# An encoder layer on one core: other Strassen product orders, sums seeded by ScalarE, and four buffers for turning the last rows

## The chip, the core and the metric

The kernel runs on one core of a Trainium2 chip. The metric is the device time of one execution in microseconds (us); lower is better. The time given is the median of three runs.

The core's engines each have an instruction queue of their own, in order: TensorE (PE: matmuls, with the weight loads listed apart as PEld), VectorE (DVE), ScalarE (ACT), GpSimd (POOL) and SyncE (SP), which here issues nearly all DMA transfers. On-chip data lies in SBUF; matmuls write PSUM, of which this kernel uses eight banks of 128 x 512 floats.

## The reference, cut

One layer of an encoder on x of 2048 rows and 1024 columns, all in float32:

```
h  = rms_norm(x, norm_mix)
z  = h @ w_in                       # q, k, v of two attentions, two gates
y_a = windowed_gqa(...)             # attention A
y_b = neighborhood_attn(...)        # attention B
merged = sigmoid(g_a + b) * (y_a @ w_proj_a) + sigmoid(g_b + b) * (y_b @ w_proj_b)
x  = x + merged @ w_out             # w_out is 1024 x 1024
h2 = rms_norm(x, norm_mlp)
x  = x + square(relu(h2 @ w_up)) @ w_down      # 1024 -> 4096 -> 1024
return rms_norm(x, norm_final)
```

## The kernel before

**Matmuls.** A float32 product is made from three reduced-precision (fp32r) matmuls: each operand is split into a high part, cast by ScalarE (L280), and a low part, a subtraction on VectorE (L281); `mm3s` (L283 to L286) issues high x high, high x low, low x high. The large products besides take one level of Strassen in Winograd's form: of an operand's four quarters, sums are made (`add`, L277, on VectorE), and seven products, numbered n = 1 to 7, replace eight. A list of orders says in which sequence the seven run; the results come from sums of products, which are kept in PSUM banks (matmuls accumulate there) or read out by VectorE and ScalarE.

**Stages on PE, in time:** the dense stage (h @ w_in, to about 365 us), attention A and B, the gated projections (to about 1175 us) with w_out beside them (its first half m=0 at about 1175 to 1250 us, its second, m=1, at about 1333 to 1418 us), up (to 2070 us), down.

**Dense stage.** `QUADS` lists its column groups; q counts them. `in_left` makes and splits the seven left operands of a group from its weights; the seven right operands, made from the normalised rows, are shared by the groups. `in_quad` (from L463) runs seven products in `ORDER`, each in two halves a of 128 columns, 12 matmuls a half. Banks are x, y, z, two each: x takes products 1 and 2, z takes 5 and 3, y takes 6, 7 and 4. Product 1 is copied out by ScalarE into c1 (L484), and VectorE adds c1 to what it reads from y and z, five adds a half (L277). A result goes through `in_result` (L440) to DRAM; if it is still in PSUM, ScalarE copies it (L454) into an `in_e` tile, of which there are two, or it is split for q and k (`qk_parts`, L423 to L430).
Beside these groups the rows x are normalised and turned for later use (squares L223, scaling L235, `turned_out`), and `wo_parts` (from L623) makes the seven right operands of w_out, split, into DRAM (wo_d).

**w_out.** `out_operands` (L1330) loads w_out's split operands back from wo_d (`pgl`, L1338, 1 MB each), and makes and splits those of the merged rows (the tiles m0 to m3). `out_products` (from L1352) runs the seven products in `ORDER_O = (1, 2, 5, 6, 7, 4, 3)`, each with four tiles t of 128 rows: product 1, once both contraction halves h are in, is copied by ScalarE into a y bank (L1378) and the rest accumulate onto it; the rows of x (`xr` tiles, from `x_row`) take the sums by VectorE's adds. Each m gives two row blocks, rows[0] and rows[1], of 512 rows. A finished block goes to DRAM (x2d), is normalised in place (`normalised`, ScalarE L223 and L235) and then turned out.

**Turning rows out.** `turned_out` (L240) takes a quarter g of a block: four 32 x 32 transposes on VectorE (L247), a multiplication by the gain (L252), and four stores of 128 KB through SP's queue (L255) into h2d, which up reads back. Its tile `ht` has one buffer. The blocks of m=0 are turned during the gated products of m=1; those of m=1 by `turned_last`: block 1 at step 6 of w_out's m=1 (in `beside_out`, L1399), block 0 after the loop (L1474 on).

**Up.** `up_start` (L1316), run beside w_out's m=1, loads up's first operands (w_up, and rows from h2d: `uraw`, `urb`). `up_right` (L1183) makes the seven right operands `ubh` (bh1 to bh7), `up_left` the left ones (`uwhla`, `uwhlb`), with sums in `uS`; `up_quad` (L1253) runs the products 1, 5, 6, 2, 7, 4, 3. `up_homes` (L1086) gives a right operand its place in SBUF, and so sets which older tiles must be done with before it can be written: bh6, bh3, bh2, rb and c are placed after the w_out loop; chunk, bh7 and bh4 after the last turned block, when w_out's tiles are closed.

**What sets the order.** The program is written as generators that run side by side (`beside`, `prep`, `started`), and a scheduler then orders each engine's queue within the dependencies, so the place of an instruction in a queue need not be that in the source. Every engine takes its queue in order: an instruction that waits holds up those behind it.

Of the kernel before, what the change touches and what calls it, by code (L numbers as in the profile page):

```python
# [92 lines left out]
def encoder_layer(ctx, tc, x, norm_mix, w_in, b_gate, sink, rpb, w_pa, w_pb, w_out,  # L93
# [275 lines left out]
    def in_left(ws, w, skip=()):  # L369
# [8 lines left out]
        for n in ORDER:  # L378
# [67 lines left out]
    def in_result(col, b, src, in_psum):  # L446
# [5 lines left out]
        if in_psum:  # L452
            t = in_e()[:, 0]
            A.copy(t, src)  # L454
            src = t
# [7 lines left out]
    def in_quad(c, w, lf, right, ybanks=ypool, zbanks=zpool):  # L463
# [4 lines left out]
        for n in ORDER:  # L468
            hl, (rh, rl) = next(lf), right[n]
            for a in range(na):  # L470
# [27 lines left out]
                elif n == 3:  # L498
                    add(V, u2[a], ps, u2[a])
                    in_result(first, 1, u2[a], False)  # L500
            yield
# [122 lines left out]
    def wo_parts(k, own):  # L624
# [5 lines left out]
        x1, x2 = rows  # L630
        b11, b12, b21, b22 = (r[:, j * BT : (j + 1) * BT] for r in rows for j in range(2))
        x3, t4 = own(), in_c()
        add(V, x3[:, 0:BT], b12, b11, ALU.subtract)
        add(V, x3[:, BT : 2 * BT], b22, b12, ALU.subtract)
        add(V, b12, b22, x3[:, 0:BT], ALU.subtract)
        add(V, t4, b21, b12, ALU.subtract)
        yield
        for ns, src in (((5, 7), x3), ((1, 6), x1), ((2, 3), x2), ((4,), t4)):
            hi = in_c() if len(ns) == 1 else in_e().rearrange("p a b -> p (a b)")
            A.copy(hi.bitcast(F32R), src)  # L640
            V.tensor_tensor(out=src.bitcast(F32R), in0=src, in1=hi, op=ALU.subtract)
            for j, n in enumerate(ns):
                for z, t in enumerate((hi, src)):
                    SY.dma_start(wo_d[n][k // 2, k % 2][:, z], t[:, j * BT : (j + 1) * BT])
# [10 lines left out]
    for q in range(2, len(QUADS)):  # L655
# [12 lines left out]
        lf = list(in_left(ws, 256, (1, 2) if q == 2 else ()))  # L668
# [8 lines left out]
        for n, _ in enumerate(quad2 if q == 2 else in_quad(*QUADS[q], iter(lf), right)):  # L677
# [638 lines left out]
    def up_start():  # L1316
# [3 lines left out]
        started.extend((rights, lf))  # L1320
# [3 lines left out]
        next(rights)  # L1324
        yield
        yield from up_left_steps(ws, lf)

    ORDER_O = (1, 2, 5, 6, 7, 4, 3)
    last_left = [None]
# [22 lines left out]
    def out_products(m, operands, rows, beside):  # L1352
# [4 lines left out]
        for n in ORDER_O:  # L1357
# [4 lines left out]
            for h in range(2):  # L1362
                l, r = ready[h]
                for t in range(4):
# [10 lines left out]
                    xc = None if n in (1, 5) else rows[i][t][:, j * BT : (j + 1) * BT]  # L1375
# [3 lines left out]
                    elif xc is not None:  # L1379
                        add(V, xc, ps, xc)  # L1380
                    if n == 7:
                        add(V, xc, z[t], xc)
                    if n in (4, 3):
                        put(x2d[2 * m + i][t * P : (t + 1) * P], rows[i][t])
                        flush(1)
            if n == 4:
                flush()
                normalised(p4x, rows[1], p4x, by_scalar=True, small=True)
        flush()
        normalised(p4x, rows[0], p4x, by_scalar=True, small=True)  # L1390

    def beside_out(m):

        loads = load_y(1) if m == 0 else up_start()
        for n in range(7):
            if n == 2 and m == 1:
# [293 lines left out]
```

## Time and profile before

| | us |
|---|---|
| median of 3 runs | 2686.42 |
| the runs | 2685.76 to 2692.47 |
| the profiled execution | 2692.09 |
| its span on the core | 2690.3 |
| PE busy | 2582.1 (96%) |
| VectorE busy | 1657.0 (62%) |
| ScalarE busy | 1258.4 (47%) |
| GpSimd busy | 352.3 (13%) |

The profile was taken of one execution, which is 5.7 us longer than the median; the 1.8 us between its span and its time lie around the span. A row of a group gives line, engine, operation, output <- input and count, then busy time, mean of one in ns, and the idle time just before with what ended it. A row of waits gives who waited for whom, then total, number and longest. A row of windows gives the stretch and its length, each engine's busy time in it with the number of instructions, the clock granted to PE (1.00 is full), the share of DMA engines busy, and GB/s. "SPq" is SP's queue issuing a DMA.

### The profile page before, as it was taken

How to read it: one execution, taken by the hardware profiler on the slowest of the kernel's cores; microseconds unless marked ns; L12 is line 12 of the kernel's file. 1: busy time of each engine (PE TensorE's matmuls, PEld its weight loads, DVE VectorE, ACT ScalarE, POOL GpSimd, SP SyncE). 2: the span in 40 equal slices, each digit the busy share in tenths (PEclk: the TensorE clock that was granted, in tenths of full speed). 3: DMA queues.
4: the chain of work that ended last, by engine and by line, in shares of the span. 5: the costliest groups of instructions: out<-in, count | busy, mean ns of one | idle time of the engine just before them, and what ended most of it. 6: DMA issues, size and time to landing. Idle time of an engine off the chain costs nothing.

```text
span 2690.3 us, 34393 instructions
## 1 busy us (share of the span) xinstructions
PE 2582.1 (96%) x12044; PEld 2142.4 (80%) x12044; DVE 1657.0 (62%) x2643; ACT 1258.4 (47%) x2245; POOL 352.3 (13%) x433
## 2 busy tenths in 40 slices
PE   7999999999999999999994999999999999999998
PEld 6878777787888888878873888888887888888887
DVE  7876756666444444466675767785666634545767
ACT  7344346666555555344343554554444233323444
POOL 0000123334555541000000000000000000000001
PEclk9999999999999999999997999999999999999999
DMA  5677685446776655777665665764435935445555
GB/s 180 228 248 202 212 284 151 118 116 174 209 228 191 195 159 150 256 242 237 227 251 160 205 214 204 253 246 145 162 114 206 347 131 172 143 149 171 179 191 170
DMA packets 351725, 525.93 MB, mean 195 GB/s; under 512 B 28584, under 2 KB 172072, under 8 KB 349376
## 3 DMA queue, kind: packets, MB, share of 16 engines
q1 hardware_dynamic: 344640, 506.95, 58.8%
q10 hardware_dynamic: 6912, 16.78, 1.7%
q8 instruction: 95, 1.56, 0.2%
q14 instruction: 78, 0.64, 0.1%
HBM read 349.51 MB, written 174.13 MB: 195 GB/s over the span
## 4 chain that ended last, share of the span: by engine, by line
PE 80%; DMA 8%; DVE 6%; ACT 2%; issue 1%; SPq 1%; POOL 0%; DVEq 0%; POOLq 0%; ACTq 0%
PE b L285 16%; PE b L286 16%; PE b L284 16%; PE mm L200 4%; PE mm L201 4%; PE mm L202 4%; PE av L984 2%; PE b L202 2%; PE b L200 2%; PE b L201 2%; PE s L945 2%; PE pt L973 2%; PE zb L284 1%; PE zb L286 1%; PE zb L285 1%
## 5 line engine op out<-in xcount | busy, mean ns | idle before, releaser
L285 PE MATMUL b<-dwh,dah 128*128 128x512 f32 x896 | 348.7, 389 | 0.4 <-DVE dwh L281 0.4
L286 PE MATMUL b<-dwh,dah 128*128 128x512 f32 x896 | 347.8, 389 | 0.0
L284 PE MATMUL b<-dwh,dah 128*128 128x512 f32 x896 | 338.3, 389 | 1.7 <-ACT dwh L280 1.7
L280 ACT CAST dah<-da 128x1024 fp32r<-128x1024 f32 (+1 forms) x128 | 120.8, 945 | 368.3 <-PE b L286 246.5
L281 DVE TENSOR_TENSOR dah<-da,dah 128x1024 fp32r<-128x1024 f32 (+1 forms) x128 | 139.2, 1089 | 216.5 <-ACT dah L280 216.3
L285 PE MATMUL b<-ubh,uwhlb 128*128 128x512 f32 x592 | 231.4, 391 | 30.6 <-DVE ubh L281 30.6
L284 PE MATMUL b<-ubh,uwhlb 128*128 128x512 f32 x592 | 231.6, 392 | 9.4 <-ACT ubh L280 7.8
L286 PE MATMUL b<-ubh,uwhlb 128*128 128x512 f32 x592 | 230.4, 391 | 0.0
L200 PE MATMUL mm<-hT,whl 128*128 128x512 f32 x544 | 218.9, 402 | 0.0
L202 PE MATMUL mm<-hT,whl 128*128 128x512 f32 x544 | 215.0, 395 | 0.0
L201 PE MATMUL mm<-hT,whl 128*128 128x512 f32 x544 | 214.3, 394 | 0.0
L284 PE MATMUL zb<-zh,zwhl 128*128 128x512 f32 x476 | 188.3, 397 | 15.7 <-DVE zc L277 8.5
L284 PEld LDWEIGHTS b<-dwh,dah 128*128 128x128 f32 x896 | 168.1, 188 | 37.0 <-ACT dwh L280 2.1
L285 PEld LDWEIGHTS b<-dwh,dah 128*128 128x128 f32 x896 | 168.2, 188 | 35.7 <-DVE dwh L281 0.8
L286 PEld LDWEIGHTS b<-dwh,dah 128*128 128x128 f32 x896 | 168.2, 188 | 34.9
L285 PE MATMUL zb<-zh,zwhl 128*128 128x512 f32 x476 | 187.4, 394 | 0.0
L286 PE MATMUL zb<-zh,zwhl 128*128 128x512 f32 x476 | 184.3, 393 | 0.8 <-DVE zwhl L281 0.8
L277 DVE TENSOR_TENSOR uc<-b,uc 128x512 f32<-128x512 f32 x160 | 109.3, 689 | 122.0 <-PE b L286 111.0
L285 PEld LDWEIGHTS b<-ubh,uwhlb 128*128 128x128 f32 x592 | 111.6, 189 | 54.6 <-DVE ubh L281 31.3
L284 PEld LDWEIGHTS b<-ubh,uwhlb 128*128 128x128 f32 x592 | 111.8, 189 | 33.6 <-ACT ubh L280 8.2
L1580 POOL TENSOR_TENSOR st<-st,power 128x1 f32<-128x1 f32 x16 | 13.6, 859 | 896.5 <-DVE st L1579 896.3
L286 PEld LDWEIGHTS b<-ubh,uwhlb 128*128 128x128 f32 x592 | 111.7, 189 | 23.1
(263 smaller groups left out, 5906.9 us busy)
## 6 DMA issues: line engine op xcount, KB each, us to landing
at<-uc SPq DMA_DIRECT2D x224, 256.0 KB
da<-at SPq DMA_DIRECT2D x96, 512.0 KB
dw<-in_w_down_dram SPq DMA_DIRECT2D x160, 256.0 KB
uraw<-in_w_up_dram SPq DMA_DIRECT2D x32, 1024.0 KB
pgl<-wo_d SPq DMA_DIRECT2D x28, 1024.0 KB
raw<-in_w_in_dram SPq DMA_DIRECT2D x34, 512.0 KB
zraw<-in_w_in_dram SPq DMA_DIRECT2D x16, 1024.0 KB
z<-zg SPq DMA_DIRECT2D x64, 256.0 KB
```

Source lines behind the costliest of these rows:

```text
L200: PE.matmul(ps, lh, rh, start=first, stop=False)
L201: PE.matmul(ps, lh, rl, start=False, stop=False)
L202: PE.matmul(ps, ll, rh, start=False, stop=last)
L277: return eng.tensor_tensor(out=out, in0=a, in1=b, op=op).ins
L280: A.copy(hi, src)
L281: return eng.tensor_tensor(out=lo, in0=src, in1=hi.bitcast(F32), op=ALU.subtract).ins
L284: PE.matmul(ps, lh, rh, start=first, stop=False, skip_group_check=True)
L285: PE.matmul(ps, lh, rl, start=False, stop=False, skip_group_check=True)
L286: PE.matmul(ps, ll, rh, start=False, stop=last, skip_group_check=True)
L945: PE.matmul(ps[:, :n], q[:, i, :], kv[:, z, B_R0[i] // 4 : (B_R0[i] + B_NR[i]) // 4, 4 * B_C0[j] : 4 * (B_C0[j] + w)], start=z == 0, stop= ...
L973: PE.transpose(pt[:kp, at + (i - i0) * P : at + (i - i0 + 1) * P], s[i][:, rr : rr + kp], ident)
L984: last = PE.matmul(po[:, i0 * P : (i0 + ni) * P], v[:kp, c, :], src[:kp, o : o + ni * P], start=first, stop=(c == 7 and z == 1), skip_grou ...
```

## The change

- **Dense stage, q = 3 to 8:** `in_quad` gives way to `in_seeded`, with the order 1, 5, 6, 2, 7, 3, 4. ScalarE copies product 1 into the y bank, onto which 6, 7 and 4 accumulate; products 5 and 6 are copied out by ScalarE (into c22 and u2); VectorE makes two adds a half instead of five. Results 2 and 4 are read from PSUM, and such copies go to `in_c` (ten buffers) instead of `in_e`. The group q = 2 keeps its order.
- **`wo_parts`:** splits each product by itself in pieces of 512 columns, its high parts in `in_c` tiles. It issues as many DMAs as before.
- **w_out:** `ORDER_O` becomes 1, 2, 5, 6, 3, 7, 4. Product 5 is added to the rows at once. Block 0 is complete after product 3, block 1 after product 4; which block is loaded and turned first follows.
- **Beside m=1:** x rows of block 1 are loaded at steps 0 and 1, up's first loads at steps 2 to 4. At step 6 block 0 is turned into four buffers, the halves of m2 and m3.
- **After the loop:** block 1 is turned through `hu`, a ring of four buffers. The homes change: bh3 is now placed after that block, and the addresses of bh2, bh3, bh4, bh7, rb, c and chunk are others. bh6 lies over m2 and m3, bh7 over the `hu` buffers, bh4 over the first of them and row tiles, bh3 over row tiles.

```diff
@@ -366,7 +366,7 @@
 
     last_part = [None]
 
-    def in_left(ws, w, skip=()):
+    def in_left(ws, w, skip=(), order=ORDER):
 
         a11, a21 = ws[0][:, :, 0:w], ws[0][:, :, w : 2 * w]
         a12, a22 = ws[1][:, :, 0:w], ws[1][:, :, w : 2 * w]
@@ -375,7 +375,7 @@
             return left_parts(src, w, eng)
 
         s1, s2 = None, None
-        for n in ORDER:
+        for n in order:
             if n in skip:
                 continue
             if n == 5:
@@ -450,7 +450,7 @@
                 SY.dma_start(dst, t)
             return
         if in_psum:
-            t = in_e()[:, 0]
+            t = in_c()
             A.copy(t, src)
             src = t
         if is_v(col):
@@ -498,6 +498,45 @@
                 elif n == 3:
                     add(V, u2[a], ps, u2[a])
                     in_result(first, 1, u2[a], False)
+            yield
+
+    ORDER_3 = (1, 5, 6, 2, 7, 3, 4)
+
+    def in_seeded(c, w, lf, right):
+
+        x, y, z = [None] * 2, [None] * 2, [None] * 2
+        u2, c22 = [None] * 2, [None] * 2
+        for n in ORDER_3:
+            hl, (rh, rl) = next(lf), right[n]
+            for a in range(2):
+                if n == 1:
+                    x[a] = zbank(xpool[a])
+                elif n == 5:
+                    z[a] = zbank(zpool[a])
+                ps = {1: x, 2: x, 5: z, 3: z, 6: y, 7: y, 4: y}[n][a]
+                at = slice(a * P, (a + 1) * P)
+                for k in range(4):
+                    mm3s(ps, hl[:, 0, k, at], hl[:, 1, k, at], rh[:, k], rl[:, k], k == 0 and n in (1, 5), k == 3)
+                first, second = c + a * P, c + w + a * P
+                if n == 1:
+                    y[a] = zbank(ypool[a])
+                    A.copy(y[a], ps)
+                elif n == 5:
+                    c22[a] = in_c()
+                    A.copy(c22[a], ps)
+                elif n == 6:
+                    u2[a] = in_c()
+                    A.copy(u2[a], ps)
+                elif n == 2:
+                    in_result(first, 0, ps, True)
+                elif n == 7:
+                    add(V, c22[a], ps, c22[a])
+                    in_result(second, 1, c22[a], False)
+                elif n == 3:
+                    add(V, u2[a], ps, u2[a])
+                    in_result(first, 1, u2[a], False)
+                elif n == 4:
+                    in_result(second, 0, ps, True)
             yield
 
     def scaled(out, ps, k):
@@ -627,21 +666,27 @@
         for p, r in enumerate(rows):
             SY.dma_start(r, w_out[0][(4 * p + k) * P : (4 * p + k + 1) * P, :])
         yield
-        x1, x2 = rows
         b11, b12, b21, b22 = (r[:, j * BT : (j + 1) * BT] for r in rows for j in range(2))
-        x3, t4 = own(), in_c()
-        add(V, x3[:, 0:BT], b12, b11, ALU.subtract)
-        add(V, x3[:, BT : 2 * BT], b22, b12, ALU.subtract)
-        add(V, b12, b22, x3[:, 0:BT], ALU.subtract)
-        add(V, t4, b21, b12, ALU.subtract)
-        yield
-        for ns, src in (((5, 7), x3), ((1, 6), x1), ((2, 3), x2), ((4,), t4)):
-            hi = in_c() if len(ns) == 1 else in_e().rearrange("p a b -> p (a b)")
+        t1, t3 = (t[:, j * BT : (j + 1) * BT] for t in (own(),) for j in range(2))
+
+        def part(n, src):
+            hi = in_c()
             A.copy(hi.bitcast(F32R), src)
             V.tensor_tensor(out=src.bitcast(F32R), in0=src, in1=hi, op=ALU.subtract)
-            for j, n in enumerate(ns):
-                for z, t in enumerate((hi, src)):
-                    SY.dma_start(wo_d[n][k // 2, k % 2][:, z], t[:, j * BT : (j + 1) * BT])
+            for z, t in enumerate((hi, src)):
+                SY.dma_start(wo_d[n][k // 2, k % 2][:, z], t)
+
+        add(V, t1, b12, b11, ALU.subtract)
+        yield
+        add(V, t3, b22, b12, ALU.subtract)
+        part(1, b11)
+        yield
+        add(V, b12, b22, t1, ALU.subtract)
+        part(3, b22)
+        yield
+        add(V, b11, b21, b12, ALU.subtract)
+        for n, src in ((2, b21), (5, t1), (7, t3), (6, b12), (4, b11)):
+            part(n, src)
             yield
 
     def own_v():
@@ -665,7 +710,7 @@
             xp = pools(s_z, "right", ("xin", "st"), "x2")
         if q == 7:
             bias_tables()
-        lf = list(in_left(ws, 256, (1, 2) if q == 2 else ()))
+        lf = list(in_left(ws, 256, (1, 2) if q == 2 else (), ORDER if q == 2 else ORDER_3))
         if q + 1 < len(QUADS):
             ws = in_weights(*QUADS[q + 1])
         if q in (5, 6):
@@ -674,7 +719,7 @@
             xt = x_tiles(xp, b, 3)
             normalised(xp, xt, Junk(), by_scalar=True)
         ops2.extend(lf if q == 2 else ())
-        for n, _ in enumerate(quad2 if q == 2 else in_quad(*QUADS[q], iter(lf), right)):
+        for n, _ in enumerate(quad2 if q == 2 else in_seeded(*QUADS[q], iter(lf), right)):
             next(prep, None)
             if q in (5, 6) and n < 4:
                 turned_out(h1d[b - 2], in_e().rearrange("p k x -> p (k x)"), xt, n)
@@ -1317,16 +1362,18 @@
 
         up_homes("raw", "whla", "whlb", "bh1", "bh5", "S")
         rights, lf = up_right(0), {}
-        started.extend((rights, lf))
+        next(rights)
+        yield
         next(rights)
         ws = up_weights(0)
         yield
-        next(rights)
-        yield
-        yield from up_left_steps(ws, lf)
-
-    ORDER_O = (1, 2, 5, 6, 7, 4, 3)
-    last_left = [None]
+        rest = up_left_steps(ws, lf)
+        started.extend((rights, lf, rest))
+        for _ in range(2):
+            next(rest)
+        yield
+
+    ORDER_O = (1, 2, 5, 6, 3, 7, 4)
 
     def out_operands(ms):
 
@@ -1372,47 +1419,44 @@
                     if h == 0:
                         continue
                     i, j = {1: (0, 0), 2: (0, 0), 5: (1, 1), 6: (0, 1), 7: (1, 1), 4: (1, 0), 3: (0, 1)}[n]
-                    xc = None if n in (1, 5) else rows[i][t][:, j * BT : (j + 1) * BT]
+                    xc = None if n == 1 else rows[i][t][:, j * BT : (j + 1) * BT]
                     if n == 1:
                         y[t] = bank_at(t)
                         A.copy(y[t], ps)
-                    elif xc is not None:
+                    else:
                         add(V, xc, ps, xc)
-                    if n == 7:
-                        add(V, xc, z[t], xc)
                     if n in (4, 3):
+                        i = int(n == 4)
                         put(x2d[2 * m + i][t * P : (t + 1) * P], rows[i][t])
                         flush(1)
-            if n == 4:
+            if n in (4, 3):
                 flush()
-                normalised(p4x, rows[1], p4x, by_scalar=True, small=True)
-        flush()
-        normalised(p4x, rows[0], p4x, by_scalar=True, small=True)
+                normalised(p4x, rows[int(n == 4)], p4x, by_scalar=True, small=True)
 
     def beside_out(m):
 
         loads = load_y(1) if m == 0 else up_start()
         for n in range(7):
-            if n == 2 and m == 1:
-                rows[1].extend(x_row(m, 1, t) for t in range(4))
-            if n in ((1, 3, 4, 6) if m == 0 else (0, 1, 3, 4)):
-                y = next(loads)
-                if m == 0:
-                    state["y"] = y
-            if m == 1 and n == 6:
-                turned_last(1)
+            if m == 0 and n in (1, 3, 4, 6):
+                state["y"] = next(loads)
+            elif m == 1:
+                if n < 2:
+                    rows[1].extend(x_row(m, 1, 2 * n + t) for t in range(2))
+                elif n < 5:
+                    next(loads)
+                elif n == 6:
+                    free = [T(p4x, [P, 2, 2, BT], F32, f"m{t}", 1).rearrange("p a b c -> p a (b c)") for t in (2, 3)]
+                    turned_last(0, lambda g: free[g // 2][:, g % 2])
             yield
-        if m == 1:
-            started.append(loads)
 
     def x_row(m, i, t):
         row0 = (2 * m + i) * BT + t * P
         return load_tile(p4x, "xr", 8, xf[row0 : row0 + P])
 
-    def turned_last(i):
+    def turned_last(i, own):
 
         for g in range(4):
-            turned_out(h2d[2 + i], T(p4x, [P, 2 * BT], F32, "ht", 1), rows[i], g, gain)
+            turned_out(h2d[2 + i], own(g), rows[i], g, gain)
 
     state = {"y": next_y}
     rows = None
@@ -1448,7 +1492,7 @@
             gated(f, 0)
         for f in range(8):
             if m:
-                i = 1 - f // 4
+                i = f // 4
                 turned_out(h2d[i], T(p4x, [P, 2 * BT], F32, "ht", 1), old[i], f % 4, gain)
             if 0 < f and f + early < 8:
                 gated(f + early, 0)
@@ -1457,7 +1501,7 @@
             if f == 3:
                 ready = [next(operands), next(operands)]
             if f >= 4 or m == 0:
-                rows[1 - f // 4].append(x_row(m, 1 - f // 4, f % 4))
+                rows[1 - f // 4 if m else f // 4].append(x_row(m, 1 - f // 4 if m else f // 4, f % 4))
         if m == 1:
             s_pg.close()
             s_w.close()
@@ -1471,16 +1515,18 @@
     for _ in beside:
         pass
     s_m.close()
-    up_homes("bh6", "bh3", "bh2", "rb", "c")
+    up_homes("bh6", "bh2", "rb", "c")
+    s_hu = ExitStack()
+    hu = ring(s_hu, "hu", [P, 2 * BT], F32, 4, "left")
     rights, lf, rest = started
     for _ in range(2):
         right = next(rights)
     for _ in rest:
         pass
-    turned_last(0)
+    turned_last(1, lambda t: hu())
+    s_hu.close()
     s_wo.close()
-
-    up_homes("chunk", "bh7", "bh4")
+    up_homes("bh7", "bh4", "bh3", "chunk")
     for m in range(2):
         if m:
             right = next(rights)
```

The orders of the queues that result differ in the dense groups q = 2 to 8 and the first part of attention A, in w_out's m=1 and in the first products of up. PE has as many instructions as before; VectorE has 2621 instructions in place of 2645, ScalarE 1989 in place of 1943; GpSimd and SP have as many as before (438 and 1525).

## The prediction

> **What bounds the kernel now.** I read the page from the top: the span, the engines, then the busy tenths in 40 slices of 67 us.
>
> ```profile
> span 2690.3 us, 34393 instructions
> ...
> PE 2582.1 (96%) x12044; PEld 2142.4 (80%) x12044; DVE 1657.0 (62%) x2643; ACT 1258.4 (47%) x2245; POOL 352.3 (13%) x433
> ...
> PE   7999999999999999999994999999999999999998
> ```
>
> PE (the matmul engine) bounds it: busy 2582.1 of 2690.3 us, so 108 us idle, and the change removes no matmul. It can win only idle PE time and the slower clock behind an idle stretch. In the slices one digit falls to 4 after the start: slice 22, about 1412 to 1480 us, where w_out ends and "up" begins. So I asked for PE's waits: total, times, longest; first over the span, then from 120 to 366 us, the dense groups q=3 to 8.
>
> ```profile
> PE b L285 <- DVE ubh L281: 32.1, 2, 30.6
> ...
> PE b L284 <- ACT ubh L280: 7.8, 1, 7.8
> PE b L284 <- DMA pgl<-wo_d: 5.0, 2, 3.2
> ```
>
> ```profile
> PE zb L284 <- DVE zc L277: 7.2, 4, 3.5
> PE zb L284 <- ACT zwhl L280: 4.2, 1, 4.2
> PE zb L395 <- ACT ze L454: 0.8, 1, 0.8
> ```
>
> Three places carry the change: the border w_out/up (30.6 + 7.8 us), the DMA wait in w_out, and 12.2 us in the dense groups.
>
> **The border first, as it holds most.** Busy time by 10-us stretches (columns: PE, PEld, DVE, ACT, POOL, granted clock, DMA share, GB/s):
>
> ```profile
> 1430.00:1440.00 10.00, 7.59 (x33) 5.59 (x31) 10.00 (x15) 7.06 (x8) 1.98 (x2) 1.00 0.59 159
> 1440.00:1450.00 10.00, 1.22 (x2) 0.50 (x2) 8.40 (x11) 3.36 (x5) 0.00 (x0) 0.63 0.92 259
> 1450.00:1460.00 10.00, 0.00 (x0) 0.00 (x0) 2.65 (x5) 0.00 (x0) 0.00 (x0) 0.50 0.47 137
> 1460.00:1470.00 10.00, 0.00 (x0) 0.00 (x0) 4.42 (x10) 0.00 (x0) 0.00 (x0) 0.50 0.34 76
> 1470.00:1480.00 10.00, 1.24 (x3) 1.05 (x4) 5.80 (x8) 0.00 (x0) 0.00 (x0) 0.50 0.39 80
> 1480.00:1490.00 10.00, 10.00 (x38) 7.98 (x38) 6.86 (x8) 5.58 (x8) 0.00 (x0) 0.82 0.80 246
> ```
>
> PE idles 2.41 + 8.78 + 10 + 10 + 8.76 = 39.95 us here; then it runs at half clock: 1.24 us x 0.5 = 0.6 and 10 x 0.18 = 1.8. Lost: **42.4 us**. VectorE is two thirds idle meanwhile. What it does stands in its timeline (start, length, instruction, idle before and who ended it) and the chain of work that ended last (start, length, what):
>
> ```profile
> 1461.57 1.42 DVE L247 STREAM_TRANSPOSE ht<-xr 128x256 f32<-128x256 f32 x4 [4.01 <-DMA h2d<-ht]
> 1463.02 1.23 DVE L252 TENSOR_TENSOR ht<-ht,gt 128x1024 f32<-128x1024 f32 x1
> 1468.19 1.43 DVE L247 STREAM_TRANSPOSE ht<-xr 128x256 f32<-128x256 f32 x4 [3.95 <-DMA h2d<-ht]
> ...
> 1477.49 2.35 DVE L281 TENSOR_TENSOR ubh<-uraw,ubh 128x1024 fp32r<-128x1024 f32 x2
> ```
>
> ```profile
> 1465.12 0.47 SPq L255
> 1465.63 2.48 DMA h2d<-ht
> ```
>
> Turning a row out takes 1.42 + 1.23 = 2.65 us of VectorE per quarter, but a quarter comes round every 1468.19 - 1461.57 = 6.62 us: `ht` is one buffer, and each quarter waits until the last of its four stores (0.47 us to issue, 2.48 to land) has landed. Both last rows go through it, eight quarters, and VectorE's queue holds the low half (L281) of product 6's operand behind them. That is the stall.
>
> **Border, after.** turned_last(0) moves to the last step of w_out, into halves of m2 and m3; turned_last(1) follows the loop, in four `hu` buffers. No quarter waits for a store any longer: a row is 4 x 2.65 = 10.6 us of VectorE instead of 4 x 6.62 = 26.5. I set t = 0 at the end of w_out on PE. Products 1 and 5 of up run first: by the rate of a full stretch (next fence: 46 matmuls in 10 us) 96 matmuls take 20.9 us. The last row's adds and scaling reach VectorE at about t = 13 (before: PE stops at about 1439 behind these two products, so w_out ended at about 1418; the last scaling was issued at 1432.45 and took 2.19 for two).
>
> ```profile
> 1420.00:1430.00 10.00, 10.00 (x46) 8.28 (x45) 4.16 (x8) 8.08 (x16) 0.55 (x1) 1.00 0.79 249
> ```
>
> ```profile
> 1432.45 2.19 ACT L235 ACTIVATE xr<-xr,st 128x1024 f32<-128x1024 f32 x2
> ```
>
> Now what is late next, product by product; all four are estimates, bounded below by 0 (the operand is there) and above by the whole row in front of it (10.6):
> - Product 6: home bh6 lies on m2/m3, free only after the 16 stores of turned_last(0): 16 x 0.47 = 7.5 us of SP's queue, plus 2.48. These begin before t = 0, so its low half is last, with part of a turned quarter (2.65) ahead: 1.7 taken.
> - Product 2: its low half stands behind the gains of the `hu` quarters: one quarter, 2.5.
> - Product 7: bh7 lies on `hu`, so its ScalarE cast (1.04) waits for the last store: 4 issues x 0.47 + 2.48 + 1.04 = 5.4, of which some 2 us lie beside product 2: 3.5.
> - Product 4: three 1.2-us VectorE steps (sums for the next weights, splits) stand ahead of its own, 3.7 in all, little covered: 4.0.
>
> Together 11.7 us, and one half-clock spell of 1.7 us (worked out below): 13.4. **Border: 13.4 - 42.4 = -29**, between -40 (next to no waits) and -17 (the four at twice the size, 23.4, and the one spell). Up's own work and the row order inside m=1 do not change the count of VectorE's adds: n=5 is now evicted at once (+4 adds), n=7 no longer adds twice (-4).
>
> **Dense groups q=3 to 8.** Each stretch below shows what a wait leaves: granted clock 0.83 over 10 us, that is 1.7 us lost on top.
>
> ```profile
> 150.00:160.00 10.00, 8.11 (x29) 6.54 (x30) 6.85 (x9) 3.04 (x4) 0.00 (x0) 0.83 0.83 282
> 275.00:285.00 10.00, 5.84 (x20) 4.79 (x21) 6.06 (x12) 4.73 (x6) 0.55 (x1) 0.83 0.79 229
> ```
>
> So they lose 12.2 + 2 x 1.7 = 15.6 us. The waits for zc L277 are PE waiting until VectorE has read a bank that PE writes next. Seeding takes the sums from VectorE: per half of a group it does 2 adds instead of 5. The price of each:
>
> ```profile
> L277 DVE TENSOR_TENSOR zc<-zb,zc 128x512 f32<-128x512 f32 x78 | 52.4, 681 | 13.6 <-PE zb L286 13.2
> ...
> L484 ACT COPY zc<-zb 128x512 f32<-128x512 f32 x12 | 7.0, 584 | 7.7 <-PE zb L286 7.7
> ```
>
> Per group VectorE loses 3 x 2 x 0.68 = 4.1 us; ScalarE copies after n=5, 6 too, and after n=4 where the result leaves as it is: 2 or 3 x 2 x 0.58 = 2.3 to 3.5 us, beside 36.5 us of matmuls (7 x 2 x 12, at 46 per 10 us). Two columns of that row matter: mean ns of one, and the idle time before it, ended by PE, so ScalarE was ready for such copies. A half-product is 12 matmuls, 2.6 us; a product is 5.2. Products 7 and 4 accumulate onto the y bank of product 6. Before, 4 follows 7, so VectorE has one half-product, 2.6 us, to read the sum; after, product 3 lies between: 7.8 us. The seed has as long (product 5 lies between it and 6). The y result leaves PSUM by one ScalarE copy into ten in_c buffers, no longer the two in_e ones that also hold the transposed rows. I leave 2.6 us for what the busier ScalarE delays (q=6, below): **-13** (from -17, all gone and the odd wait in q=2, to -5, where only the zc waits shrink by half and the clock stays). wo_parts splits seven 512-wide pieces instead of three of 1024 and one of 512: about 3 x 0.1 us more each, off PE's path in the same slack. 0.
>
> **w_out.** m=0 keeps its order: 0. In m=1, the chain shows a 1-MB load of a split w_out operand behind the four 1-MB loads for up:
>
> ```profile
> 1338.82 13.97 DMA pgl<-wo_d
> ```
>
> ```profile
> 1340.00:1350.00 10.00, 9.66 (x43) 7.68 (x41) 7.14 (x7) 7.12 (x10) 0.00 (x0) 1.00 1.03 385
> 1350.00:1360.00 10.00, 7.17 (x24) 5.57 (x24) 10.00 (x9) 3.98 (x4) 0.00 (x0) 0.83 0.86 334
> ```
>
> The DMA engines are full (1.03), PE then waits 3.2 us and gets 1.7 us less clock. The change puts up's loads at steps 2 to 4, behind this one: 4.9 us go. Against it: VectorE is at 10.00 of 10 just there, and each product's adds (0.68 each) now follow at once; 1 us of new wait. **-4** (from -7, with the small waits of the same place, to +2, were the later loads of up to arrive late).
>
> **A rule and a row.** The Trainium skill (page "TensorE: Matmul & The Clock Gate", Part 1: The HAM clock gate) says that the clock falls to half after an idle window of about 3.4 us and returns after as long a busy one. By it my two longer leftover waits at the border (3.5 and 4.0 us) would draw a spell each and the two shorter none: the sum would be 1.7 us worse than with the one spell that I took.
>
> What the trace shows is less kind: one 1.8-us wait for pgl in m=0, and yet 0.84 of the clock. So up to four spells, 6.8 us, belong in my bound.
>
> ```profile
> 1190.00:1200.00 10.00, 8.16 (x30) 6.04 (x29) 5.77 (x6) 2.00 (x2) 0.00 (x0) 0.84 0.83 325
> ```
>
> **Sum.** -29 - 13 - 4 = -46. Attention, gating, the rest of up, and down are unchanged: 0. The profiled execution took 2692.1 us (1.8 beyond its span of 2690.3); it becomes 2646, span 2644. It lies 5.7 us above the median of the runs, 2686.4; from that the same sum gives about **2640 us**.
>
> **Rivals.**
> 1. *The stall only moves.* Homes bh7, bh4 and bh3 lie on `hu` and on the row tiles, so up's operands still wait for stores. If row and stores run one behind the other: 10.6 + 16 x 0.47 + 2.5 + 2.2 (cast and low half) = 22.8, product 4's 4.0 and two spells 3.4: 30 lost, so the border gives -12, in all -29: **2657**. For it: both rows' 32 stores pass SP's one queue at 0.47 us each, the later loads of up behind them. Against: two products, 21 us, run beside it. 0.16.
> 2. *Full cover.* Border leaves 3 us (-39), dense -16, w_out -7: -62, **2624**. For it: VectorE's 28 us of row and operands fits in four products, 42 us. Against: the two queues are in order and the homes chain them. 0.16.
> 3. *Slower: seeds late on ScalarE.* A seed stands in ScalarE's queue; if what is ahead of it waits, product 6 waits. q=6 shows the pattern: squares of the next rows stand ahead of a cast, which PE awaits.
>
> ```profile
> 264.91 0.63 ACT L223 ACTIVATE ze<-xin 128x512 f32<-128x512 f32 x1 [5.22 <-DVE zS L277]
> ...
> 278.11 1.03 ACT L280 CAST zwhl<-zraw 128x1024 fp32r<-128x1024 f32 x1
> ```
>
> ScalarE is taken for 13 us there. A lag of L costs L - 7.8 per group; over six groups it outweighs the 13 + 33 gained from L = 7.8 + 46/6 = 15.5; at 18 us it is 6 x 10.2 = 61, so +15: **2701**. Against: these rows are normalised in only two of the six groups. 0.04.
> 4. *It does not do what it says at the border:* the row's quarters are spread over the buffers but VectorE and SP still take them ahead of everything and wait on the same stores; only 13 + 4 are gained: **2669**; without the dense gain as well, 2682, no change. 0.06, of which 0.02 for no change.
>
> **How the numbers follow.** Forecast 0.58, rival 1 0.16, rival 2 0.16, rival 3 0.04, rival 4 0.06. A measurement of this kernel can tell about 0.3%, 8 us, from no change. Faster by more: 0.58 + 0.16 + 0.16 + 0.04 = 0.94, less 0.01 for a mix of small gains: 0.93; within: 0.03; slower: 0.04. The forecast's own bounds are -17 - 5 + 2 = -20 at worst and -64 at best, not all at once; 2617 to 2665 takes in the forecast, rivals 1 and 2, and leaves out 3, 4 and the tails, under 2 in 10.
>
> **What would show it.** Border: PE busy 8 or more in every 10-us stretch behind the first two up products, no clock of 0.50 over a whole stretch, no VectorE wait for a store of `hu`; rival 1 shows ScalarE's bh7 cast ended by DMA h2d with more than 8 us of PE idle. Dense: no PE wait for zc L277 over 1 us from 120 to 366 us; rival 3 shows PE waiting for ScalarE's copies in the y bank. w_out: no wait for pgl near 1350 us, PE clock 1.00. The prediction is wrong if the last row's scaling comes much later than t = 13, or if up's later left operands, no longer prepared before the loop's end, become the new wait.

## The result, and the profile after

The changed kernel takes 2664.07 us in the median of four runs (2660.27 to 2668.93). Four runs of the kernel before gave a median of 2688.19 us, so the change saves 24 us: ratio 0.991, with a 95% interval of 0.9888 to 0.9931. The forecast was 2640 us in a range of 2617 to 2665. The direction was right, and half the size came.

The page of the changed kernel: span, engines, PE's busy tenths, granted clock.

```profile
span 2663.0 us, 34440 instructions
...
PE 2584.8 (97%) x12044; PEld 2143.4 (80%) x12044; DVE 1635.8 (61%) x2619; ACT 1274.8 (48%) x2291; POOL 348.5 (13%) x433
...
PE   7989989999999999999998999999999999999998
...
PEclk9999998999999999999998999999999999999999
```

The 4 in slice 22 is an 8: the long stall is gone. But slices 3 and 6 (133 to 200 and 333 to 399 us), 9 before, are 8 now, and in the clock a new 8 stands in slice 7 (about 400 to 465 us), the start of attention A, where nothing was expected. PE's longest waits after, but for one of 7.6 us in the kernel's first part that was there before as well (7.3 us):

```profile
PE zb L284 <- ACT zb L523: 7.3, 1, 7.3
PE b L284 <- ACT ubh L280: 6.9, 2, 5.7
PE mm L200 <- ACT hT L753: 4.6, 1, 4.6
...
PE b L284 <- DVE uc L277: 3.3, 1, 3.3
```

The second and fourth are what is left of the border. The first is a seed of the dense stage (L523 is `A.copy(y[a], ps)`), the third lies at attention's start: both are new.

**Where the 27 us of the two profiled executions lie** (2692.09 and 2664.86 us). The matmuls are as many in both, so I compared the start of the one with the same number, stage by stage. Columns: what was forecast, what the traces show.

| stage | forecast | trace |
|---|---|---|
| first 30 us (the code there is the same) | 0 | -1.6 |
| dense stage, to 358 us | -13 | -5.8 |
| end of the dense stage and attention | 0 | +10.8 |
| w_out, m=0 | 0 | -2.0 |
| w_out, m=1 | -4 | -3.8 |
| border and up | -29 | -24.8 |
| sum | -46 | -27.2 |

w_out's m=1 and the border came nearly as forecast. The dense part of the change, forecast to give 13 us, cost 5 (-5.8 + 10.8). The -1.6 and the -2.0 can't be put down to the change: in the first 30 us the code is the same, and dense_only below, whose w_out is that of before, shows -2.7 in m=0.

### The profile page after: what moved, and what is told of

Same layout as the page of the kernel before. It is cut to its first block, busy times and chain, and to the rows that moved or that the text cites. A ratio compares the mean times of both kernels' runs of the same rounds, so it can differ in the third digit from the quotient of the medians.

```text
span 2663.0 us, 34440 instructions
## 1 busy us (share of the span) xinstructions
PE 2584.8 (97%) x12044; PEld 2143.4 (80%) x12044; DVE 1635.8 (61%) x2619; ACT 1274.8 (48%) x2291; POOL 348.5 (13%) x433
## 4 chain that ended last, share of the span: by engine, by line
PE 78%; DMA 9%; DVE 7%; ACT 2%; issue 2%; SPq 1%; POOL 0%; POOLq 0%; ACTq 0%; DVEq 0%
PE b L285 15%; PE b L284 15%; PE b L286 15%; PE mm L200 4%; PE mm L201 4%; PE mm L202 4%; PE av L1029 2%; PE b L200 2%; PE b L201 2%; PE b L202 2%; PE pt L1018 2%; PE s L990 2%; PE zb L286 1%; PE zb L284 1%; PE zb L285 1%
## 5 line engine op out<-in xcount | busy, mean ns | idle before, releaser
L200 PE MATMUL mm<-hT,whl 128*128 128x512 f32 x544 | 219.8, 404 | 4.6 <-ACT hT L753 4.6
L202 PE MATMUL mm<-hT,whl 128*128 128x512 f32 x544 | 215.6, 396 | 0.0
L285 PEld LDWEIGHTS b<-ubh,uwhlb 128*128 128x128 f32 x592 | 112.4, 190 | 25.2 <-DVE ubh L281 1.7
L200 PEld LDWEIGHTS mm<-hT,whl 128*128 128x128 f32 x544 | 103.0, 189 | 23.2 <-ACT hT L753 5.2
```

The costliest lines, as they stand in the source:

```text
L200: PE.matmul(ps, lh, rh, start=first, stop=False)
L202: PE.matmul(ps, ll, rh, start=False, stop=last)
L285: PE.matmul(ps, lh, rl, start=False, stop=False, skip_group_check=True)
```

## The experiments

Times are medians; "before" is the kernel before, run on the same chip beside each batch (2689.69, 2689.22, 2688.52, 2689.91 us in the order of the batches). Ratios are to it, with 95% intervals.

| kernel | us | ratio (interval) |
|---|---|---|
| border_only | 2658.71 | 0.9886 (0.9871 to 0.9901) |
| dense_only | 2695.44 | 1.0023 (1.0014 to 1.0033) |
| seed_dve | 2663.50 | 0.9906 (0.9889 to 0.9922) |
| hu_one | 2677.85 | 0.9956 (0.9941 to 0.9971) |
| kb_old | 2657.87 | 0.9879 (0.9864 to 0.9893) |
| dist_pool | 2663.04 | 0.9901 (0.9886 to 0.9915) |
| border_hu_pool | 2671.46 | 0.9932 (0.9917 to 0.9947) |
| wo_old | 2656.27 | 0.9879 (0.9863 to 0.9896) |
| wo_early | 2648.85 | 0.9854 (0.9839 to 0.9868) |
| kb_wo_early | 2644.48 | 0.9834 (0.9820 to 0.9849) |
| kb_wo_old | 2652.45 | 0.9867 (0.9849 to 0.9885) |
| hu_two | 2644.59 | 0.9837 (0.9824 to 0.9850) |

The changed kernel's own interval is 0.9888 to 0.9931. Those of kb_old and wo_old just overlap it, so the 6 and 8 us that they gain on it below are less sure than the 15 us of wo_early.

**The two halves.** border_only is the changed kernel with the dense stage of before; dense_only is the reverse.

```diff
-  lf = list(in_left(ws, 256, ..., ORDER if q == 2 else ORDER_3))
+  lf = list(in_left(ws, 256, ...))
-  ... in_seeded(*QUADS[q], iter(lf), right)
+  ... in_quad(*QUADS[q], iter(lf), right)
   (wo_parts and the tile for copies in in_result as before; dense_only: all this the other way round)
```

> The changed kernel with the dense stage as before (products in the old order by in_quad, wo_parts in 1024-wide pieces, result copies in in_e); w_out, its turned rows and up as in the change. Theory 1 (the whole gain is made at w_out and its border, -2, -4 and -25 us in the profiles; the dense stage's 6 us are given back at the start of attention): about 31 us faster than before, 2655 to 2659 us, 5 to 8 us faster than the changed kernel, and attention A at the same times as before. Rival (the prediction: the dense stage is worth 13 us and attention nothing): slower than the changed kernel, near 2675 us.

> The kernel before with the dense part of the change alone (in_seeded for q=3 to 8, wo_parts in 512-wide pieces, copies in in_c); w_out and up as before. Theory 1: PE waits for a seed at about 173 us (some 7 us and a half-clock spell), the dense stage ends about 6 us early, attention A's start is about 6 us late, in all +2 to +7 us against before: 2689 to 2694 us. Rival (the prediction): -13 us, 2674 us.

border_only is 31.0 us faster than before, dense_only 5.8 us slower (1.4 us beyond what was expected); together -25.2, against -24.1 of the whole change. Theory 1 holds: the gain is w_out and border, and the dense part loses. In border_only attention starts within 1 us of its time before; in dense_only its start is late as in the changed kernel.

**Buffers or places?** hu_one leaves one `hu` buffer.

```diff
-    hu = ring(s_hu, "hu", [P, 2 * BT], F32, 4, "left")
+    hu = ring(s_hu, "hu", [P, 2 * BT], F32, 1, "left")
```

> The changed kernel with one hu buffer instead of four; all homes, orders and the first turned block as in the change. Theory 1 (the buffers set the time of the last block): its four quarters come round every 6.6 us again, bh7 waits for the last of them, PE stands still 10 to 16 us longer in front of product 7, the clock falls as well: 2674 to 2684 us. Rival (the earlier place of block 0 and the new homes make the gain): within 3 us of the changed kernel.

14 us come back. Its VectorE timeline shows the old round trip again, here 7.07 us from one quarter to the next, each started by the landing of the one before; PE's wait in front of product 7 is 25.2 us in place of 5.7:

```profile
1448.99 1.43 DVE L247 STREAM_TRANSPOSE hu<-xr 128x256 f32<-128x256 f32 x4 [6.69 <-DMA h2d<-hu]
1450.45 1.23 DVE L252 TENSOR_TENSOR hu<-hu,gt 128x1024 f32<-128x1024 f32 x1
1456.06 1.42 DVE L247 STREAM_TRANSPOSE hu<-xr 128x256 f32<-128x256 f32 x4 [4.38 <-DMA h2d<-hu]
```

```profile
PE b L284 <- ACT ubh L280: 26.5, 2, 25.2
```

So of the 25 us at the border some 14 are the four buffers; the rest is block 0's earlier place and the other edits there, which were not taken apart.

**The seed that waits.** ScalarE's timeline in the changed kernel suggested why the seed was late: it is behind casts of the keys of attention B (L425), which wait for a `ze` buffer to be stored.

```profile
177.38 1.06 ACT L425 CAST ze<-zb 128x512 fp32r<-128x512 f32 x1 [3.59 <-DMA ks_b<-ze]
178.24 1.07 ACT L280 CAST zwhl<-zraw 128x1024 fp32r<-128x1024 f32 x1
179.60 0.57 ACT L523 COPY zb<-zb 128x512 f32<-128x512 f32 x1 [0.30 <-DVE ze L426]
```

seed_dve takes the seed of that one group to VectorE.

```diff
-                    A.copy(y[a], ps)
+                    if c == O_VB:
+                        V.tensor_copy(out=y[a], in_=ps)
+                    else:
+                        A.copy(y[a], ps)
```

> The changed kernel with one thing altered: in the group behind the keys of attention B (q=4, from about 165 us) VectorE copies product 1 into the y bank, not ScalarE, so that these two seeds do not stand behind ScalarE's casts that wait for the stores of ks_b. Theory 1 (that queue is what PE waits for): the wait of 7.3 us and its half-clock spell of 6.8 us (3.4 us lost) go, the dense stage ends 7 to 11 us earlier; the start of attention, which by the theory waits for transfers, takes some of it back, so 0 to 10 us in the time. Rival (product 6's operands or the y bank itself are late): the wait stays over 4 us.

The wait stays. In seed_dve PE waits for the cast itself, and VectorE's seed (`zb<-zb`) starts only after the cast and the subtraction of a result that lies in PSUM (`ze<-zb`):

```profile
PE zb L284 <- ACT ze L425: 6.9, 1, 6.9
```

```profile
179.68 1.09 DVE L426 TENSOR_TENSOR ze<-zb,ze 128x512 fp32r<-128x512 f32 x1 [3.28 <-ACT ze L425]
180.87 0.70 DVE L524 COPY zb<-zb 128x512 f32<-128x512 f32 x1
```

Theory 1 falls here: not the queue but the bank is late. With the new order, result 4 of the keys stays in the y bank until one of two `ze` buffers has been stored; before, VectorE's add took it into an in_c tile. kb_old gives this one group its old order and adds back.

```diff
-        lf = list(in_left(..., ORDER if q == 2 else ORDER_3))
+        lf = list(in_left(..., ORDER if q in (2, 3) else ORDER_3))
-        ... in_seeded(*QUADS[q], iter(lf), right)
+        ... (in_quad if q == 3 else in_seeded)(*QUADS[q], iter(lf), right)
```

> The changed kernel with one group of the dense stage as before: the keys of attention B (q=3) use the old product order and in_quad; all other groups are seeded. Theory 2 (the wait at 173 us is for the y bank: result 4 of the keys stays in it until one of the two ze buffers has been stored; VectorE's seed did not help): the wait of 7 us and its spell go, the old wait of some 4 us near 148 us comes back, the dense stage ends 4 to 9 us earlier than in the changed kernel. If attention A starts when its own loads are there, the time stays within 3 us of the changed kernel; if it starts when the dense stage ends, 2655 to 2660 us. Rival: the wait stays.

6 us faster than the changed kernel. From 120 to 185 us PE's waits for results are down to one:

```profile
PE zb L284 <- DVE zc L277: 1.8, 1, 1.8
```

The dense stage of kb_old ends 13 us ahead of before, as much as was forecast, but attention gives it all back: VectorE's first softmax step is at 391.8 us, before at 391.1.

**Attention's start.** PE in three kernels from 380 to 420 us; first the kernel before, then the changed one, then wo_early (below):

```profile
380.00:400.00 20.00, 15.98 (x70) 13.46 (x69) 6.00 (x23) 7.26 (x23) 8.20 (x13) 0.91 1.09 317
400.00:420.00 20.00, 17.49 (x93) 14.04 (x92) 15.29 (x54) 15.62 (x49) 8.41 (x15) 1.00 0.83 229
```

```profile
380.00:400.00 20.00, 12.71 (x43) 8.61 (x43) 6.08 (x16) 5.32 (x9) 5.57 (x8) 0.82 1.10 350
400.00:420.00 20.00, 15.89 (x59) 12.64 (x59) 13.05 (x48) 14.64 (x51) 8.79 (x17) 0.66 0.77 178
```

```profile
380.00:400.00 20.00, 17.11 (x82) 12.86 (x82) 12.90 (x44) 12.40 (x38) 11.42 (x19) 1.00 1.11 326
400.00:420.00 20.00, 19.54 (x107) 15.76 (x106) 16.18 (x50) 16.52 (x45) 9.00 (x15) 1.00 0.79 227
```

The changed kernel does 102 matmuls in these 40 us where before did 163, at a clock of 0.82 and 0.66. The first softmax step of attention needs the bias, made by GpSimd from the table `dist`. In the changed kernel SP issues that load at 390.94 us and GpSimd waits for it. VectorE waits 0.26 us for GpSimd, but first 7.29 us for ScalarE, in front of another instruction (L409) that stands ahead in its queue:

```profile
390.94 0.59 SPq L793 DMA_DIRECT2D dist<-in_dist_a_dram  x1
```

```profile
396.66 4.17 POOL L799 TENSOR_SCALAR biasa<-dist 128x384 f32<-128x384 f32 x8 [2.29 <-DMA dist<-in_dist_a_dram]
```

```profile
396.26 0.69 DVE L409 TENSOR_TENSOR z<-mm,z 128x512 fp32r<-128x512 f32 x1 [7.29 <-ACT z L408]
397.21 0.48 DVE L831 CUSTOM_DVE_ANT_0 sa<-s,biasa,sink_t 128x256 f32<-128x256 f32 x1 [0.26 <-POOL biasa L799]
```

Before, the same load was issued at 384.79 us. dist_pool issues it from GpSimd's queue.

```diff
-    SY.dma_start(dist, dist_a)
+    G.dma_start(dist, dist_a)
```

> The changed kernel with one load issued by another engine: the table of distances, which attention A's bias is made from, by GpSimd in place of SyncE, whose queue reached it at 391 us behind stores that wait (385 us before). Theory (the first scores wait for an entry late in SyncE's queue): attention A's start moves 5 to 8 us earlier, 2656 to 2660 us. Rival (the DMA engines are full from 360 to 400 us, and the next load binds as late): within 3 us of the changed kernel.

No gain: GpSimd issues it at 387.12 us only, 3.8 us sooner, and there too the load waits. The tile `dist` takes memory of the `xin` tiles from which wo_parts stores its pieces, so the last such stores have to be read out first, whoever issues the load: in dist_pool's trace the semaphores of the last two (issued at 379.30 and 380.06 us) are full at 385.66 and 386.37 us, and GpSimd's waits for them end 0.03 us later. (The tile view names `ka<-ks_a` for this wait; that load uses another of the six semaphores that GpSimd waited for.) In the changed kernel the last ones go from 379.68 us, in the kernel before at 366 us. The load alone does not set the start, though: in dist_pool GpSimd begins the bias 3 us sooner (393.61 us), and the first softmax step only 1.3 us sooner (395.96 us), right behind L409 again. Two kernels change the pieces: wo_old takes the old wo_parts, wo_early the new pieces in fewer steps.

```diff
 wo_early:
         add(V, t1, b12, b11, ALU.subtract)
-        yield
         add(V, t3, b22, b12, ALU.subtract)
         part(1, b11)
         yield
...
-        yield
         add(V, b11, b21, b12, ALU.subtract)
-        for n, src in ((2, b21), (5, t1), (7, t3), (6, b12), (4, b11)):
-            part(n, src)
+        yield
+        for ns in (((2, b21), (5, t1)), ((7, t3), (6, b12)), ((4, b11),)):
+            for n, src in ns:
+                part(n, src)
             yield
```

> The changed kernel with wo_parts as before (1024-wide pieces, high parts in ze), the seeded groups kept. It asks which of the two parts of the dense change makes attention A late. Theory (the seeded groups: the dense stage ends sooner than its stores and attention's loads get through): attention late as in the changed kernel, and the ze buffers more contended, 2664 to 2672 us. Rival (the smaller pieces put w_out's last stores among attention's loads at 376 to 381 us): attention starts as in the kernel before, 2655 to 2660 us.

> The changed kernel with wo_parts' seven 512-wide pieces finished three steps sooner (three steps of two pieces or fewer in place of seven of one), so that in the last group none is left for after the last product. Theory (the pieces left over at the end stand among attention A's first loads and hold them up): PE's wait for hT near 380 us shrinks, attention A's start moves 6 to 12 us earlier than in the changed kernel, 2652 to 2659 us. Rival (it is the sum of transfers and the busier in_c buffers, wherever the pieces stand): within 3 us of the changed kernel.

Both are faster than the changed kernel, by 8 and 15 us (wo_early by more than expected), and both start attention in time: the first softmax step is at 383.2 and 381.8 us. For wo_old the rival, not my theory, was right: the pieces, not the seeded groups, made attention late. In wo_early the last `xin` store is issued at 363.32 us, `dist` at 369.99, and the first softmax step comes 15 us sooner:

```profile
369.99 0.51 SPq L793 DMA_DIRECT2D dist<-in_dist_a_dram  x1
```

```profile
381.80 0.48 DVE L831 CUSTOM_DVE_ANT_0 sa<-s,biasa,sink_t 128x256 f32<-128x256 f32 x1 [1.17 <-PE s L830]
```

That the pieces cause it is shown by wo_early. How they do so is open. The late `dist` load is one candidate. The other is the order of the queues, which the scheduler makes otherwise in wo_early: most of attention's first scores stand among the last `hT` products (L200 to L202) rather than behind them, and no L409 stands in front of the first softmax step. dist_pool, where the load moved and that order stayed, speaks for the second; the two were not separated.

In wo_old the dense stage itself gains nothing (it ends 0.6 us after before): its seeds wait for ScalarE, 7.4 us in three places, probably because wo_parts again takes the `ze` buffers. With the new pieces the changed kernel ends it 7.4 us ahead: they do help the dense groups; only their end was badly placed.

**Put together.**

> wo_early and kb_old together. If the two causes are separate their gains add: 6 us for the keys' group and what wo_early gives, 2645 to 2653 us. If the start of attention A takes back whatever the dense stage gains: as wo_early.

> kb_old and wo_old together: wo_parts and the keys' group as before, the other five groups seeded. wo_old still waited 4 us at 180 us for the bank that the keys' results held, and its seeds 7.4 us in all for ScalarE: that wait goes, 4 to 6 us faster than wo_old, 2650 to 2653 us, attention A's start as in the kernel before. Rival (the waits for ScalarE's seeds stay, since wo_parts uses the ze buffers): as wo_old, 2656 us.

kb_wo_early (the two diffs above in one) is 44 us faster than before, 20 more than the change: the fastest arrangement beside hu_two. The gains of kb_old and wo_early nearly add (6.2 and 15.2 us alone, 19.6 together). kb_wo_old lies 4 us ahead of wo_old, with intervals that overlap: there too the keys' group seems to cost something, 2 us less than by kb_old.

**The rest of the border.** border_hu_pool has the last block's 16 stores issued by GpSimd.

```diff
-            turned_out(h2d[2 + i], own(g), rows[i], g, gain)
+            turned_out(h2d[2 + i], own(g), rows[i], g, gain, G if i else None)
```

> border_only with the stores of the last turned block issued by GpSimd's queue, not SyncE's. Theory (up's loads stand behind these 16 stores, which wait for the gains): the load for product 4 is issued some 10 us earlier, the wait in front of product 4 and its half-clock spell go (4 us), the wait for bh7 in front of product 7 stays: 4 to 6 us faster than border_only, 2653 to 2656 us. Rival (the stores from GpSimd land later, bh7 is written later): no gain, or a few us slower.

13 us slower than border_only. GpSimd needed from 1427.92 to 1452.64 us for the 16 stores, with pauses between them for which the trace names nothing, though the last gain on VectorE was done at 1432.2 us; SyncE took 10.1 us for them in border_only.

```profile
1427.92 1.97 POOL L255 DMA_DIRECT2D h2d<-hu  x3 [6.41 <-DVE hu L252]
1433.62 1.74 POOL L255 DMA_DIRECT2D h2d<-hu  x3 [3.74 <-issue]
...
1452.05 0.59 POOL L255 DMA_DIRECT2D h2d<-hu  x1 [0.80 <-issue]
```

hu_two is kb_wo_early with the 16 stores shared by SyncE and ScalarE.

```diff
-            (queue or SY).dma_start(...)
+            (queue[a % 2] if queue else SY).dma_start(...)
-            turned_out(h2d[2 + i], own(g), rows[i], g, gain)
+            turned_out(h2d[2 + i], own(g), rows[i], g, gain, (SY, A) if i else None)
```

> kb_wo_early with the 16 stores of the last turned block issued by SyncE and ScalarE in turn. Theory (bh7's cast waits for the last of 16 stores that one queue issues one by one, and the load for product 4 stands behind them): the stores are out 3 to 5 us sooner, the wait of about 6.5 us in front of product 7 shrinks to 2 to 4 us and its half-clock spells with it, 3 to 6 us faster than kb_wo_early: 2638 to 2642 us. Rival (the gains before the stores set the time, or ScalarE's issues hold up its casts): within 2 us of kb_wo_early.

The same time as kb_wo_early (0.9837 and 0.9834, intervals over each other). Half the stores on SyncE took 8.89 us, where all 16 on that queue took 10.29 in kb_wo_early, so one queue's issuing was not the limit alone:

```profile
1413.25 8.89 SPq L255 DMA_DIRECT2D h2d<-hu  x8
```

```profile
1415.83 10.29 SPq L255 DMA_DIRECT2D h2d<-hu  x16
```

What sets their pace is open; the first gains on VectorE (3.5 us for three) account for part only.

## Why the prediction was right, and why only by half

The median lies 0.9 us inside the upper end of the range (2665). That it lies inside is partly luck: the border's half of the forecast held, the dense half failed, and none of the four rivals described what came instead.

**Border: right in mechanism, 4 us too good.** Forecast -29, trace -24.8. The round trip through one buffer made the larger part of the stall, as hu_one shows (14 of 25 us); what block 0's earlier place gave was not measured by itself. Of the signs named, two came (no stretch at a clock of 0.50, no wait of VectorE for a store of `hu`) and one did not: PE is busy 4.88 and 6.68 of 10 us in two stretches. The waits left after are 11.0 us by PE's busy time below (1.73 + 0.88 + 5.12 + 3.32), against 11.7 forecast:

```profile
1420.00:1430.00 10.00, 8.27 (x30) 6.12 (x29) 9.24 (x17) 8.76 (x12) 1.52 (x1) 0.86 0.65 184
1430.00:1440.00 10.00, 9.12 (x37) 6.76 (x36) 10.00 (x10) 4.58 (x6) 0.00 (x0) 0.97 0.90 251
1440.00:1450.00 10.00, 4.88 (x11) 3.40 (x12) 7.13 (x7) 5.41 (x7) 0.00 (x0) 0.71 0.94 257
1450.00:1460.00 10.00, 6.68 (x23) 5.11 (x22) 9.38 (x10) 2.79 (x5) 0.00 (x0) 0.84 1.02 381
1460.00:1470.00 10.00, 10.00 (x42) 8.17 (x41) 5.57 (x7) 5.20 (x9) 0.00 (x0) 0.93 0.29 109
```

Product by product the estimates were less good: product 6 waits 1.7 us (1.7 forecast), 2 waits 0.3 (2.5), 7 waits 5.7 (3.5), 4 waits 3.3 (4.0); that the sum agrees is luck. The term mis-sized is the clock: one spell of 1.7 us was taken, but the granted clocks 0.86, 0.97, 0.71, 0.84 and 0.93 cost up to 10 x (0.14 + 0.03 + 0.29 + 0.16 + 0.07) = 6.9 us (a little less, since a spell costs nothing while PE stands still). The prediction had the row that said so (1.8 us of waiting in w_out's m=0, and a clock of 0.84) and used it for the bound only.

One step was wrong in itself without harm to the sum: the stall in before stood in front of product 7, not 6. A product of up here is 24 matmuls, some 5.3 us (the prediction's 96 are four), so the 21 us between the end of w_out and PE's stop held three and a half products, not two; the first half of product 1 had run ahead of w_out's last matmuls.

**w_out: right.** Moving up's loads behind the split operand took the wait away: -3.8 in m=1, -4 forecast.

**Dense groups: the slack was counted, the exit was not.** That a seed has 7.8 us, one and a half products, was true and did not matter. The step that failed is "The y result leaves PSUM by one ScalarE copy into ten in_c buffers": the keys and queries do not go that way, they are split straight from PSUM into `ze`, and for the keys of B that buffer is tied up by stores. kb_old, with this one group undone, takes that wait away and ends the dense stage 13 us early; that five seeded groups there give what was forecast for six is partly luck. Rival 3 (a seed late on ScalarE) had the right symptom in one group of six but the wrong cause, by seed_dve; in wo_old, where seeds wait in three places, neither cause was told apart.

**Attention, "unchanged: 0", and wo_parts, "off PE's path in the same slack. 0".** This is the larger failure: +10.8 us. wo_parts was costed by its durations on ScalarE and VectorE (0.1 us a piece), and those are hidden. What was left out is that it went from four splitting steps to seven, so that the last pieces of the last group fell behind its last product, into the start of attention, and that the memory of their tiles is what attention's first table is loaded into. wo_early, with the same pieces three steps earlier, takes 15 us back. Most of the loss is clock: from 380 to 420 us PE idles 11.4 us (6.5 before), and by the granted clock it loses up to 20 x 0.18 + 20 x 0.34 = 10.4 us (1.8 before). Together that is 13.5 us, as the matmuls' starts say too (7.4 us ahead of before at 380 us, 6.1 behind at 420); 2.7 us come back in the rest of attention.

With both faults mended (kb_wo_early) the kernel takes 2644 us, 4 us from the forecast. Stage by stage that is less exact: its border gives 27.7 us and w_out's m=1 3.8, as forecast, but its dense stage 7.8 in place of 13; 5 us more come from attention and m=0, which the forecast had at nothing.

## What to carry to other kernels

When a sum is moved from an add into SBUF to an accumulation in PSUM, ask for each result how it leaves the bank and what that exit waits for: a result that was free to go may now hold the bank that the next group needs. When work is cut into more steps in a side generator, count the steps against the loop that drives it, and look which tiles the last ones keep alive and what is loaded over them. A stall that turns into several short ones keeps much of its price in the clock.

## What the runs showed of the hardware

A granted clock below 1.00 followed waits shorter than 3 us. In the changed kernel PE lost 1.73 us between 1420 and 1430 us, in two pauses of 1.2 and 0.5 us, and the clock there is 0.86. In the kernel before, a single wait of 1.9 us stands in a stretch with a clock of 0.91 (440 to 460 us), while one of 2.6 us left it at 1.00 (355 to 375 us): the length of a pause does not decide alone. At attention's start (380 to 420 us above), where PE has much to wait for but no pause beyond 5 us, it is 0.82 and 0.66 over 20 us each.

The Trainium skill (page "TensorE: Matmul & The Clock Gate", Part 1: The HAM clock gate) says that the half rate comes after an idle window of about 3.4 us, and that the window runs freely. These rows do not bear the first half out: no pause in that stretch at the border is near 3.4 us long, and the clock fell. The measurement decides: short pauses must be counted as able to draw a spell.

The same 16 stores of 128 KB took 10.1 us from SyncE's queue (border_only) and 24.7 us from GpSimd's (border_hu_pool); SyncE and ScalarE together took 8.9 us (hu_two), hardly less than SyncE alone (10.3 us in kb_wo_early).
